# Six of eight blocks of the boundary unit computed ahead of the norm instead of eight

## The chip, the cores and the metric

The kernel runs on one core of a Trainium2 chip. The metric is the device time of one execution in microseconds (us), as the median of the runs. TensorE is called PE here, VectorE DVE, ScalarE ACT, GpSimd POOL and SyncE SP, as the profile calls them.

## The reference

The program is a small encoder trunk: two layers on 256 grid tokens and 16 meta tokens (272 columns), 1024 channels. Each layer is a half-step SwiGLU feed-forward block (FFN), a token mixer (neighbourhood attention in layer 0, differential attention in layer 1) and a second FFN, each between two norms:

```python
h = h + 0.5 * rmsnorm(swiglu(rmsnorm(h, g[0]), gate, up, down), g[1])
h = h + rmsnorm(mixer(rmsnorm(h, g[2])), g[3])
h = h + 0.5 * rmsnorm(swiglu(rmsnorm(h, g[4]), gate, up, down), g[5])
```

where `rmsnorm(x, g) = x * rsqrt(mean(x*x) + 1e-6) * g`, and `swiglu` is `(silu(x @ gate) * (x @ up)) @ down` with an inner width of 2816. Six sub-layers make five boundaries. At each, the output f of one sub-layer must be normed and added to h before the next sub-layer's first projection can use the new h.

## The kernel before

Channels lie on the 128 partitions, tokens on the free axis, so an activation is 8 blocks of 128 x 272. Every float32 matrix product is made of three passes on PE: each operand is split into a rounded high part and the rest (`whi`, `wlo` for weights, `xhi`, `xlo` for activations), and PE adds hi·hi, lo·hi and hi·lo. A *unit* is one 128-column slice of a weight matrix: 8 blocks, 24 matmuls (`mm3` for each block). There are 328 units; each is loaded by a DMA that SP issues, ACT makes its high part (line 126) and DVE its low part (line 132). Seven units can be held split (`W_BUFS`); `pump` splits the next one only if the unit seven before it was declared finished by `done()`.

The order on PE is the program's own everywhere; in the FFNs that holds for all engines, in the two attentions the other engines are ordered by a scheduler, which goes by the order of the code and by what each instruction waits for.

A boundary works so. The sub-layer's last product comes out in 8 blocks; `Post.feed` squares each one (ACT, line 268), scales it by its gain (`fg`, DVE), adds the squares up on POOL (`sqa`, line 273), and makes a split copy `fhi`, `flo` of it with the next gain. Meanwhile `input_hi` and `input_lo` make `xhi`, `xlo` from the old h. Since the norm is one factor per token, the first unit of the next sub-layer, here called unit 0, can be computed before it is known: once from the old h (pass A, into the bank `ab[0]`) and once from f (pass B, into `ab[1]`), 24 matmuls each. `enter` issues both. Between their blocks stand two steps of the norm: `post.rstd` (PE sums `sqa` over the channels into `st`, line 242; DVE makes v, line 250; POOL makes r, line 257) and `post.spread` (PE spreads r over the partitions, line 263). Then `post.add` goes over the 8 blocks: DVE scales f (line 350) and adds it to h (line 357), ACT makes the new `xhi` (line 277) and its square, DVE the new `xlo` (line 280), POOL adds the squares. PE's next five units follow as a *group*, block by block (`proj_group`, lines 200, 201 and 204: 15 matmuls for a block), so that block k only needs the new `xhi[k]` and `xlo[k]`. Ahead of the group's block 6 stands `ir.begin`, the sum of all eight new squares (line 242 again), and ahead of block 7 `ir.end` (line 263), which ACT copies out as `r2` (line 305). Unit 0's sum, pass A plus the scaled pass B, is formed by lines 383 to 385 (`u0`).

The five boundaries lie at 213 us (FFN to neighbourhood attention), 349 us (to an FFN), 558 us (FFN to FFN), 764 us (FFN to differential attention) and 902 us (to the last FFN, with 256 columns). The text calls them 1 to 5.

Of the kernel before, what the change touches and what calls it, by code (L numbers as in the profile page):

```python
# [38 lines left out]
W_BUFS = 7  # L39
RAW_BUFS = 5  # L40
WO_GROUP = 3
LEAD = 6
WARM = 8
FIRST = 2
# [3 lines left out]
def encoder_kernel(ctx, tc, xT, wall, gT, bqkvT, boT, sublnT, rpbP, metab, lam_p, rel,  # L48
# [16 lines left out]
    def nm(s):  # L65
        uid[0] += 1
        return f"{s}_{uid[0]}"
# [107 lines left out]
    def done(n=1):  # L175
        count["done"] += n
# [12 lines left out]
            mm3(acc[:, :n], w[0][:, k, :], w[1][:, k, :], ihi[:, k, :n], ilo[:, k, :n], k == 0, k == KB - 1)  # L189
        done()  # L190

    def proj_group(units, n_of, ihi, ilo, accs, hook):

        ws = [next_unit() for _ in units]
        for k in range(KB):
            if k in hook:
                hook[k]()
            for j in range(len(units)):
                n = n_of(units[j])
                nc.tensor.matmul(accs[j][:, :n], ws[j][0][:, k, :], ihi[:, k, :n], start=k == 0, stop=False)  # L200
                nc.tensor.matmul(accs[j][:, :n], ws[j][1][:, k, :], ihi[:, k, :n], start=False, stop=False)  # L201
            for j in range(len(units)):
                n = n_of(units[j])
                nc.tensor.matmul(accs[j][:, :n], ws[j][0][:, k, :], ilo[:, k, :n], start=False, stop=k == KB - 1)  # L204
        done(len(units))


    first = [load((2, 2, 4)) for _ in range(FIRST)]
# [98 lines left out]
    class Post:  # L307
# [8 lines left out]
        def open(self):  # L316
            self.cm = tc.tile_pool(name=nm("fx"), bufs=1, side="right")
            pool = self.cm.__enter__()
            self.fhi = pool.tile([P, KB, T], F32R, tag="fhi", name=nm("fhi"))
            self.flo = pool.tile([P, KB, T], F32R, tag="flo", name=nm("flo"))  # L320

        def feed(self, m, ps):
            n = self.n
            f = fg[:, m, :n]
            pump_hi() if m < KB - 1 else None
            if self.bias is None:
                sq = square(ps, n)
                nc.vector.tensor_scalar(out=f, in0=ps, scalar1=self.gain[:, m:m + 1], scalar2=None, op0=ALU.mult)
            else:
                sq = square(ps, n, bias=self.bias[:, m:m + 1])  # L330
                nc.vector.tensor_scalar(out=f, in0=ps, scalar1=self.bias[:, m:m + 1],
                                        scalar2=self.gain[:, m:m + 1], op0=ALU.add, op1=ALU.mult)
            self.acc = sq if m == 0 else add_squares(self.acc, sq, n)
            g = self.gain_next[:, m:m + 1]
            fhi = self.fhi[:, m, :n]
            nc.scalar.activation(fhi, f, AF.Copy, scale=g)
            pump_lo()
            nc.vector.scalar_tensor_tensor(out=self.flo[:, m, :n], in0=f, scalar=g, in1=fhi.bitcast(F32),
                                           op0=ALU.mult, op1=ALU.subtract)
# [23 lines left out]
    def enter(post, n_of, ab, rest):  # L363

        n0 = n_of(0)
        w = next_unit()
        for k in range(KB):
            if k == post.ready:  # L370
                post.rstd()
            mm3(ab[0][:, :n0], w[0][:, k, :], w[1][:, k, :], xhi[:, k, :n0], xlo[:, k, :n0], k == 0, k == KB - 1)
        for k in range(KB):
            if k == 2:
                post.spread()
            mm3(ab[1][:, :n0], w[0][:, k, :], w[1][:, k, :], post.fhi[:, k, :n0], post.flo[:, k, :n0],
                k == 0, k == KB - 1)
        done()
        post.cm.__exit__(None, None, None)
        ir = InputRstd(post.n_next)  # L380
        post.add(ir)
        u0 = nrm.tile([P, T], F32, tag="u0", name=nm("u0"), bufs=1)
        nc.scalar.copy(u0[:, :n0], ab[1][:, :n0])
        nc.vector.tensor_tensor(out=u0[:, :n0], in0=u0[:, :n0], in1=post.bc[:, :n0], op=ALU.mult)
        nc.vector.tensor_tensor(out=u0[:, :n0], in0=ab[0][:, :n0], in1=u0[:, :n0], op=ALU.add)
        pump(1)
        proj_group(range(1, 1 + len(rest)), n_of, xhi, xlo, rest, {6: ir.begin, 7: ir.end})
        pump(1)
        return [u0] + rest, ir

    def gains(l, i):
        return g_sb[:, l * 6 + i, :]
# [27 lines left out]
    def ffn(l, which, n, before, gain_next, n_next, extra=()):  # L420
        extra = list(extra)
        with all_banks(), tc.manual_schedule():
# [6 lines left out]
            with tc.tile_pool(name=nm("ffn"), bufs=1) as fp:  # L429
                mhi = fp.tile([P, FT, T], F32R, tag="mhi", name=nm("mhi"))  # L430
                mlo = fp.tile([P, FT, T], F32R, tag="mlo", name=nm("mlo"))

                def evac(f, pg, pu):
                    gt = ft.tile([P, T], F32, tag="gt", name=nm("gt"))
                    ut = ft.tile([P, T], F32, tag="ut", name=nm("ut"))
                    nc.vector.tensor_tensor(out=gt[:, :n], in0=pg[:, :n], in1=r2[:, :n], op=ALU.mult)  # L436
                    nc.vector.tensor_tensor(out=ut[:, :n], in0=pu[:, :n], in1=r2[:, :n], op=ALU.mult)
                    nc.scalar.activation(gt[:, :n], gt[:, :n], AF.Silu)  # L438
                    pump_hi()
                    nc.vector.tensor_tensor(out=ut[:, :n], in0=gt[:, :n], in1=ut[:, :n], op=ALU.mult)  # L440
                    pump_lo()
                    nc.scalar.copy(mhi[:, f, :n], ut[:, :n])
                    nc.vector.tensor_tensor(out=mlo[:, f, :n], in0=ut[:, :n],
                                            in1=mhi[:, f, :n].bitcast(F32), op=ALU.subtract)
                    pump(1)

                with tc.tile_pool(name=nm("fft"), bufs=2) as ft:
                    pools["tmp"] = ft
                    for f in range(3):
                        evac(f, accs[2 * f], accs[2 * f + 1])  # L450
                    for f in range(3, FT):
                        a, b = acc_tile(), acc_tile()
                        proj(a, n, xhi, xlo)
                        proj(b, n, xhi, xlo)
                        evac(f, a, b)
                        if extra:
                            extra.pop(0)()
                    if which == 0:
                        nc.scalar.activation(warm, ones, AF.Exp)
                        if l == 1:  # L460
                            lambda_scalar()
                if gain_next is None:
                    with tc.tile_pool(name="last", bufs=1) as lp:
                        last_down(lp, mhi, mlo)
                    return None
                post = Post(n, half_gains(l, 1 if which == 0 else 5), None, gain_next, n_next, 6)
                post.open()
                w = None
                for m in range(KB):
                    ps = acc_tile()  # L470
                    for f in range(FT):
                        idx = m * FT + f
                        if idx % KB == 0:
                            if w is not None:
                                done()
                            w = next_unit()
                            if extra:
                                extra.pop(0)()
                            if idx % FT < 16:
                                pump(1)  # L480
                        mm3(ps[:, :n], w[0][:, idx % KB, :], w[1][:, idx % KB, :],
                            mhi[:, f, :n], mlo[:, f, :n], f == 0, f == FT - 1)
                    post.feed(m, ps[:, :n])
                    if m < KB - 1:
                        for i in range(m + m // 6, m + 1 + (m + 1) // 6):
                            input_hi(i, gain_next, n_next)
                            input_lo(i, gain_next, n_next)
                assert not extra
                done()
            return post  # L490
# [204 lines left out]
    def natten(l, b4, before, gain_next, n_next):  # L695
        with ExitStack() as outer, ExitStack() as inner:
# [172 lines left out]
                    single.append((i, lambda p=pairs, go=go: go(p)))  # L869
            for u in range(6):  # L870
                stage(u, accs[u])
            post = Post(T, gains(l, 3), bo_sb, gain_next, n_next, 7)
            fl = Filler(range(6, 24), lambda u: T, stage, ohi, olo, post)
            pipeline(fl, steps, (1, 3, 6), single)
            nc.gpsimd.tensor_tensor(out=warm[:NMETA], in0=meta["L"][:, 0, 0:1], in1=cur["sm"][:NMETA, 0:1], op=ALU.add)
# [5 lines left out]
    class Filler:  # L881
# [5 lines left out]
        def run(self, units, n_of, staging, ohi, olo, post):  # L887
# [13 lines left out]
            for k in range(KB):  # L901
                for j in range(WO_GROUP):
                    mm3(self.outs[j][:, :n], ws[j][0][:, k, :], ws[j][1][:, k, :],
                        ohi[:, k, :n], olo[:, k, :n], k == 0, k == KB - 1)
                    if k < KB - 1 or j < WO_GROUP - 1:
                        yield
                if k < KB - 1:
                    for i in range(k + k // 6, k + 1 + (k + 1) // 6):
                        input_hi(i, post.gain_next, post.n_next)
                        input_lo(i, post.gain_next, post.n_next)  # L910
            done(WO_GROUP)
            yield

# [41 lines left out]
    def diff_attention(l, b4, before, gain_next, n_next):  # L955
# [3 lines left out]
        with ExitStack() as outer, ExitStack() as inner:  # L959
# [122 lines left out]
            nc.vector.tensor_scalar(out=r2s[0], in0=ir.r2[:, :NG], scalar1=0.125, scalar2=None, op0=ALU.mult)  # L1082
            for u in range(6):
                stage(u, accs[u])
            post = Post(NG, gains(l, 3), None, gain_next, n_next, 7)
# [113 lines left out]
```

## Time and profile before

| | |
|---|---|
| median of 3 runs | 1104.18 us (1103.87 to 1104.58) |
| profiled execution | 1104.21 us |
| its span, first to last instruction | 1102.4 us |
| PE busy | 1089.8 us (99%), 8492 matmuls |
| DVE busy | 779.9 us (71%) |
| ACT busy | 612.6 us (56%) |
| POOL busy | 131.9 us (12%) |
| mean granted TensorE clock | 0.995 |

The profiled execution takes 1.8 us more than its span, which lie around it. Busy times are shares of the span. Matmuls overlap: one is shown with some 0.29 us, but the next begins 0.125 us after it, so the starts are to be read, not the lengths.

### The profile page before, as it was taken

Reading aid. Unit: us, or ns where it says so; the run is one execution under the profiler, and the core shown is the slowest. Engines: PE = TensorE matmul, PEld = TensorE weight load, DVE = VectorE, ACT = ScalarE, POOL = GpSimd, SP = SyncE. Lnnn points to the kernel's source line nnn. Section 1 sums busy time; section 2 is a strip of 40 time slices with the busy share of each in tenths; the row PEclk is TensorE's granted clock in tenths of the full one; section 3 lists DMA queues with packets and bytes.
Section 4 is the critical chain, followed back from the end, with each engine's and each line's share of the span. In section 5 each row is a group of like instructions: output and inputs, shape, how many; then the busy total and the mean of one; then the engine's idle time right before and its main releaser. Section 6 shows DMA issues by size and latency. Waiting matters only on the chain.

```text
span 1102.4 us, 22240 instructions
## 1 busy us (share of the span) xinstructions
PE 1089.8 (99%) x8492; PEld 1057.4 (96%) x8492; DVE 779.9 (71%) x1669; ACT 612.6 (56%) x1398; POOL 131.9 (12%) x234
## 2 busy tenths in 40 slices
PE   8999999999999999999999999999999999999997
PEld 8999999999989999999999999999999999999986
DVE  6676868687677887675578766666887778877642
ACT  4554655476666564455546544554677865654541
POOL 4000001152222200000020000001321122000000
PEclk8999999999999999999999999999999999999999
DMA  7589985525334375695526555555253343755551
GB/s 252 178 151 212 275 228 168 176 73 182 110 97 135 110 224 172 178 239 192 175 69 210 192 185 164 181 184 172 77 173 96 111 140 113 241 184 185 184 167 39
DMA packets 64956, 181.79 MB, mean 165 GB/s; under 512 B 13960, under 2 KB 22192, under 8 KB 64848
## 3 DMA queue, kind: packets, MB, share of 16 engines
q1 hardware_dynamic: 64848, 180.35, 54.4%
q8 instruction: 67, 1.10, 0.4%
q14 instruction: 41, 0.34, 0.1%
HBM read 179.21 MB, written 1.20 MB: 164 GB/s over the span
## 4 chain that ended last, share of the span: by engine, by line
PE 90%; DVE 6%; issue 2%; ACT 1%; POOL 0%; DMA 0%; SPq 0%; POOLq 0%; DVEq 0%; ACTq 0%
PE acc L179 16%; PE acc L181 15%; PE acc L180 15%; PE att L179 10%; PE att L181 9%; PE att L180 9%; DVE xlo L280 1%; DVE wlo L132 1%; DVE h L357 1%; PE acc L200 1%; PE acc L204 1%; PE acc L509 1%; PE acc L511 1%; PE acc L510 1%; PE acc L201 1%
## 5 line engine op out<-in xcount | busy, mean ns | idle before, releaser
L132 DVE TENSOR_TENSOR wlo<-raw,whi 128x512 fp32r<-128x512 f32 (+1 forms) x660 | 439.0, 704 | 64.3 <-ACT whi L126 60.9
L126 ACT CAST whi<-raw 128x512 fp32r<-128x512 f32 (+1 forms) x660 | 374.4, 613 | 107.4 <-issue 44.3
L179 PE MATMUL acc<-xhi,whi 128*128 128x272 f32 (+1 forms) x1016 | 299.2, 294 | 0.0
L181 PE MATMUL acc<-xlo,whi 128*128 128x272 f32 (+1 forms) x1016 | 291.9, 287 | 0.0
L180 PE MATMUL acc<-xhi,wlo 128*128 128x272 f32 (+1 forms) x1016 | 291.0, 286 | 0.0
L179 PEld LDWEIGHTS acc<-xhi,whi 128*128 128x128 f32 x1016 | 191.4, 188 | 5.6 <-issue 3.7
L180 PEld LDWEIGHTS acc<-xhi,wlo 128*128 128x128 f32 x1016 | 191.5, 188 | 0.2 <-DVE wlo L132 0.2
L181 PEld LDWEIGHTS acc<-xlo,whi 128*128 128x128 f32 x1016 | 191.3, 188 | 0.0
L179 PE MATMUL att<-xhi,whi 128*128 128x272 f32 (+1 forms) x560 | 161.1, 288 | 0.0
L181 PE MATMUL att<-xlo,whi 128*128 128x272 f32 (+1 forms) x560 | 160.9, 287 | 0.0
L180 PE MATMUL att<-xhi,wlo 128*128 128x272 f32 (+1 forms) x560 | 160.3, 286 | 0.0
L438 ACT ACTIVATE gt<-gt 128x272 f32<-128x272 f32 (+1 forms) x88 | 37.7, 428 | 143.7 <-DVE gt L436 143.7
L179 PEld LDWEIGHTS att<-xhi,whi 128*128 128x128 f32 x560 | 105.5, 188 | 0.7 <-issue 0.7
L181 PEld LDWEIGHTS att<-xlo,whi 128*128 128x128 f32 x560 | 105.5, 188 | 0.0
L180 PEld LDWEIGHTS att<-xhi,wlo 128*128 128x128 f32 x560 | 105.4, 188 | 0.0
L179 PE MATMUL acc<-mhi,whi 128*128 128x272 f32 x286 | 82.8, 290 | 0.0
L181 PE MATMUL acc<-mlo,whi 128*128 128x272 f32 x286 | 82.3, 288 | 0.0
L180 PE MATMUL acc<-mhi,wlo 128*128 128x272 f32 x286 | 82.3, 288 | 0.0
L273 POOL TENSOR_TENSOR sqa<-sqa,sq 128x272 f32<-128x272 f32 (+1 forms) x66 | 55.6, 842 | 166.7 <-ACT sq L268 163.8
L179 PE MATMUL att<-mhi,whi 128*128 128x272 f32 x242 | 70.1, 290 | 0.0
L181 PE MATMUL att<-mlo,whi 128*128 128x272 f32 x242 | 69.7, 288 | 0.0
L180 PE MATMUL att<-mhi,wlo 128*128 128x272 f32 x242 | 69.6, 288 | 0.0
(248 smaller groups left out, 1970.2 us busy)
## 6 DMA issues: line engine op xcount, KB each, us to landing
raw<-wall SPq DMA_DIRECT2D x326, 512.0 KB, 4.0
bias<-tab SPq DMA_DIRECT2D x8, 320.0 KB, 9.9
bias<-tab SPq DMA_DIRECT2D x8, 256.0 KB
h<-xT SPq DMA_DIRECT2D x3, 272.0 KB, 4.6
out<-ht SPq DMA_DIRECT2D x3, 256.0 KB
raw<-wall SPq DMA_DIRECT2D x4, 128.0 KB, 3.1
raw<-wall SPq DMA_DIRECT2D x2, 256.0 KB
grow<-glast SPq DMA_DIRECT2D x1, 512.0 KB, 5.1
```

What stands on the lines that cost most here:

```text
L126: nc.scalar.copy(split[i][0][:, sl], raw[i][:, sl])
L132: nc.vector.tensor_tensor(out=wlo[:, sl], in0=raw[i][:, sl], in1=whi[:, sl].bitcast(F32), op=ALU.subtract)
L179: nc.tensor.matmul(ps, whi_k, mhi, start=first, stop=False)
L180: nc.tensor.matmul(ps, wlo_k, mhi, start=False, stop=False)
L181: nc.tensor.matmul(ps, whi_k, mlo, start=False, stop=last)
L200: nc.tensor.matmul(accs[j][:, :n], ws[j][0][:, k, :], ihi[:, k, :n], start=k == 0, stop=False)
L201: nc.tensor.matmul(accs[j][:, :n], ws[j][1][:, k, :], ihi[:, k, :n], start=False, stop=False)
L204: nc.tensor.matmul(accs[j][:, :n], ws[j][0][:, k, :], ilo[:, k, :n], start=False, stop=k == KB - 1)
L273: nc.gpsimd.tensor_tensor(out=t[:, :n], in0=acc[:, :n], in1=sq[:, :n], op=ALU.add)
L280: nc.vector.scalar_tensor_tensor(out=xlo[:, m, :n], in0=h[:, m, :n], scalar=gain[:, m:m + 1], in1=xhi[:, m, :n].bitcast(F32), op0=ALU.mult ...
L357: nc.vector.tensor_tensor(out=h[:, m, :n], in0=h[:, m, :n], in1=fg[:, m, :n], op=ALU.add)
L438: nc.scalar.activation(gt[:, :n], gt[:, :n], AF.Silu)
```

## The change

`AHEAD = 6`. Passes A and B cover blocks 0 to 5 alone, 18 matmuls each. Blocks 6 and 7 of unit 0 are computed once, from the new h, in the group: its blocks 6 and 7 have 18 matmuls instead of 15, and they go on adding into the bank of pass A. `fhi`, `flo` and the old `xhi`, `xlo` are no longer made for blocks 6 and 7. `rstd` stands two blocks earlier in pass A (before block 4 after an FFN, 5 after an attention, instead of 6 and 7), `spread` before block 3 of pass B instead of 2. `done()` for unit 0 comes with the group's, and the last addition of `u0` stands behind the group.

```diff
-    def proj_group(units, n_of, ihi, ilo, accs, hook):
-        ws = [next_unit() for _ in units]
+    def proj_group(units, n_of, ihi, ilo, accs, hook, begun=()):
+        parts = [(w, acc, n, AHEAD) for w, acc, n in begun]
+        parts += [(next_unit(), acc, n_of(u), 0) for u, acc in zip(units, accs)]
         for k in range(KB):
             if k in hook:
                 hook[k]()
...
+            here = [p for p in parts if k >= p[3]]
+            for w, acc, n, _ in here:
+                nc.tensor.matmul(acc[:, :n], w[0][:, k, :], ihi[:, k, :n], start=k == 0, stop=False)
+                nc.tensor.matmul(acc[:, :n], w[1][:, k, :], ihi[:, k, :n], start=False, stop=False)
+            for w, acc, n, _ in here:
+                nc.tensor.matmul(acc[:, :n], w[0][:, k, :], ilo[:, k, :n], start=False, stop=k == KB - 1)
+        done(len(parts))
...
             self.acc = sq if m == 0 else add_squares(self.acc, sq, n)
+            if m >= AHEAD:
+                pump_lo()
+                return
...
-        for k in range(KB):
+        for k in range(AHEAD):
             if k == post.ready:
                 post.rstd()
-            mm3(ab[0][:, :n0], ..., k == 0, k == KB - 1)
-        for k in range(KB):
-            if k == 2:
+            mm3(ab[0][:, :n0], ..., k == 0, False)
+        for k in range(AHEAD):
+            if k == 3:
                 post.spread()
-            mm3(ab[1][:, :n0], ..., k == 0, k == KB - 1)
-        done()
+            mm3(ab[1][:, :n0], ..., k == 0, k == AHEAD - 1)
...
         nc.vector.tensor_tensor(out=u0[:, :n0], in0=u0[:, :n0], in1=post.bc[:, :n0], op=ALU.mult)
+        pump(1)
+        proj_group(range(1, 1 + len(rest)), n_of, xhi, xlo, rest, {6: ir.begin, 7: ir.end}, [(w, ab[0], n0)])
         nc.vector.tensor_tensor(out=u0[:, :n0], in0=ab[0][:, :n0], in1=u0[:, :n0], op=ALU.add)
-        pump(1)
-        proj_group(range(1, 1 + len(rest)), n_of, xhi, xlo, rest, {6: ir.begin, 7: ir.end})
         pump(1)
```

What the change does to the order is shown at three places (the changed kernel's lines stand one to six further on). First PE at boundary 3, where the group comes to block 6; `st` is the sum of the squares, the bank `acc_7313`, then `acc_7277`, that of unit 1. Before:

```order
L204 MATMUL att_7317<-xlo,whi_7268 128x272
L242 MATMUL st_7542<-ones,sqa_7436 128x1 x3
L200 MATMUL acc_7313<-xhi,whi_7130 128x272
L201 MATMUL acc_7313<-xhi,wlo_7131 128x272
L200 MATMUL att_7314<-xhi,whi_7162 128x272
```

and now:

```order
L206 MATMUL att_7281<-xlo,whi_7234 128x272
L244 MATMUL st_7493<-ones,sqa_7388 128x1 x3
L203 MATMUL acc_7275<-xhi,whi_7070 128x272
L204 MATMUL acc_7275<-xhi,wlo_7071 128x272
L203 MATMUL acc_7277<-xhi,whi_7100 128x272
```

Unit 0 (`acc_7275`, the bank of pass A) now leads the block behind the sum; the same stands at the other four boundaries.

Next DVE at the same boundary, behind `post.add`; `u_586` is `u0`, v the second sum's, `gt` the FFN's first evacuation. Before:

```order
L384 TENSOR_TENSOR u_586_7440<-u_586_7440,st_7336 128x272
L385 TENSOR_TENSOR u_586_7440<-acc_7311,u_586_7440 128x272
L132 TENSOR_TENSOR wlo_7445<-raw_7136,whi_7444 128x512 x2
L250 TENSOR_SCALAR v_7543<-st_7542 128x3
L132 TENSOR_TENSOR wlo_7586<-raw_7168,whi_7585 128x512 x2
L436 TENSOR_TENSOR gt_7601<-u_586_7440,r_590_7568 128x272
```

and now:

```order
L388 TENSOR_TENSOR u_586_7392<-u_586_7392,st_7294 128x272
L133 TENSOR_TENSOR wlo_7396<-raw_7106,whi_7395 128x512 x2
L252 TENSOR_SCALAR v_7494<-st_7493 128x3
L391 TENSOR_TENSOR u_586_7392<-acc_7275,u_586_7392 128x272
L133 TENSOR_TENSOR wlo_7544<-raw_7138,whi_7543 128x512 x2
L440 TENSOR_TENSOR gt_7559<-u_586_7392,r_590_7522 128x272
```

The addition that frees the bank of pass A has moved from ahead of the second sum to behind it, and reads what the group's last block writes.

Last ACT at boundary 4, from the copy of `r2` on; `hi` are the high parts of the first query (x256) and the first key (x272). Before:

```order
L305 COPY r_732_10120<-st_10094 128x272
L987 CAST hi_10157<-qk_10155 128x256
L126 CAST whi_10214<-raw_9766 128x512 x2
L126 CAST whi_10301<-raw_9796 128x512 x2
L987 CAST hi_10163<-qk_10161 128x272
```

and now:

```order
L307 COPY r_732_10060<-st_10031 128x272
L127 CAST whi_10081<-raw_9678 128x512 x2
L127 CAST whi_10158<-raw_9721 128x512 x2
L127 CAST whi_10245<-raw_9748 128x512
L989 CAST hi_10101<-qk_10099 128x256
L127 CAST whi_10245<-raw_9748 128x512
L127 CAST whi_10267<-raw_9780 128x512 x2
L127 CAST whi_10307<-raw_9939 128x512
L989 CAST hi_10107<-qk_10105 128x272
```

Ahead of the first key's high part stand nine casts of weights instead of four. Two of the nine are those of the unit that takes over unit 0's buffers (`whi_10081`); before, they stood within `post.add`. At boundary 1 two casts have moved in the same way.

## Rows read from the trace of the kernel before

**Rows 1.** The page: TensorE's busy time, its granted clock in 40 slices, the chain.

```profile
PE 1089.8 (99%) x8492; PEld 1057.4 (96%) x8492; DVE 779.9 (71%) x1669; ACT 612.6 (56%) x1398; POOL 131.9 (12%) x234
...
PEclk8999999999999999999999999999999999999999
...
PE 90%; DVE 6%; issue 2%; ACT 1%; POOL 0%; DMA 0%; SPq 0%; POOLq 0%; DVEq 0%; ACTq 0%
```

**Rows 2.** The waits of PE: total us, times, longest us.

```profile
PE st L242 <- POOL sqa L273: 1.7, 4, 0.6
...
PE att L1076 <- DVE A L1017: 1.0, 1, 1.0
```

**Rows 3.** Timeline of PE at boundary 3: start us, length us, instruction, [idle before].

```profile
558.53 0.28 PE L179 MATMUL acc<-xhi,whi 128*128 128x272 f32 x1
...
560.79 0.28 PE L242 MATMUL st<-ones,sqa 128*128 128x1 f32 x2
...
562.97 0.27 PE L263 MATMUL st<-ident,r 128*128 128x128 f32 x1
...
565.55 0.29 PE L200 MATMUL acc<-xhi,whi 128*128 128x272 f32 x1
...
577.30 0.27 PE L242 MATMUL st<-ones,sqa 128*128 128x1 f32 x1 [0.28 <-POOL sqa L273]
...
582.17 0.28 PE L179 MATMUL acc<-xhi,whi 128*128 128x272 f32 x1
```

**Rows 4.** Timeline of POOL, DVE and ACT at boundary 3.

```profile
559.33 0.78 POOL L273 TENSOR_TENSOR sqa<-sqa,sq 128x272 f32<-128x272 f32 x1 [7.26 <-ACT sq L268]
...
561.79 0.86 POOL L257 TENSOR_TENSOR r<-v,mhalf 128x3 f32<-128x3 f32 x1 [1.68 <-DVE v L250]
...
563.49 0.44 DVE L350 TENSOR_TENSOR fg<-fg,st 128x272 f32<-128x272 f32 x1 [1.78 <-PE st L263]
...
564.50 0.53 ACT L277 ACTIVATE xhi<-h,g_sb 128x272 fp32r<-128x272 f32 x1 [4.23 <-DVE h L357]
...
576.48 0.77 POOL L273 TENSOR_TENSOR sqa<-sqa,sq 128x272 f32<-128x272 f32 x1 [1.38 <-ACT sq L268]
```

**Rows 5.** Timeline of ACT, POOL and PE at boundary 2.

```profile
350.43 0.53 ACT L336 ACTIVATE fhi<-fg,g_sb 128x272 fp32r<-128x272 f32 x1 [0.93 <-DVE fg L331]
...
351.48 0.77 POOL L273 TENSOR_TENSOR sqa<-sqa,sq 128x272 f32<-128x272 f32 x1 [0.91 <-ACT sq L268]
...
352.31 0.27 PE L242 MATMUL st<-ones,sqa 128*128 128x1 f32 x1 [0.52 <-POOL sqa L273]
...
354.33 0.32 PE L263 MATMUL st<-ident,r 128*128 128x128 f32 x1
```

**Rows 6.** Timeline of PE at boundary 5.

```profile
904.70 0.28 PE L242 MATMUL st<-ones,sqa 128*128 128x1 f32 x2
...
906.24 0.32 PE L263 MATMUL st<-ident,r 128*128 128x128 f32 x1
```

**Rows 7.** Timeline of POOL, PE and ACT at boundary 1.

```profile
213.72 0.78 POOL L273 TENSOR_TENSOR sqa<-sqa,sq 128x272 f32<-128x272 f32 x1
...
215.13 0.28 PE L242 MATMUL st<-ones,sqa 128*128 128x1 f32 x2
...
217.31 0.27 PE L263 MATMUL st<-ident,r 128*128 128x128 f32 x1
...
219.06 0.53 ACT L277 ACTIVATE xhi<-h,g_sb 128x272 fp32r<-128x272 f32 x1 [4.09 <-DVE h L357]
...
219.89 0.29 PE L200 MATMUL acc<-xhi,whi 128*128 128x272 f32 x1
...
220.55 0.36 ACT L383 COPY u<-att 128x272 f32<-128x272 f32 x1
```

**Rows 8.** Timeline of ACT, DVE and PE behind boundary 4.

```profile
786.28 0.41 ACT L987 CAST hi<-qk 128x256 fp32r<-128x256 f32 x1 [1.02 <-DVE qk L981]
786.59 2.18 ACT L126 CAST whi<-raw 128x512 fp32r<-128x512 f32 x4
788.67 0.41 ACT L987 CAST hi<-qk 128x272 fp32r<-128x272 f32 x1
...
789.12 0.44 DVE L989 TENSOR_TENSOR lo<-qk,hi 128x272 fp32r<-128x272 f32 x1
...
790.21 0.40 PE L179 MATMUL att<-hi,hi 64*128 64x272 f32 x2
```

More of the change, by code (lines that the diff above doesn't have):

```diff
@@ L41 @@
 WO_GROUP = 3
+AHEAD = 6
 LEAD = 6
@@ L197, in proj_group @@
                 hook[k]()
[L198 to L205, printed above, removed]
+            here = [p for p in parts if k >= p[3]]
[5 more added lines that the diff above has]
+        done(len(parts))
     first = [load((2, 2, 4)) for _ in range(FIRST)]
@@ L318, in open @@
             pool = self.cm.__enter__()
-            self.fhi = pool.tile([P, KB, T], F32R, tag="fhi", name=nm("fhi"))
-            self.flo = pool.tile([P, KB, T], F32R, tag="flo", name=nm("flo"))
+            self.fhi = pool.tile([P, AHEAD, T], F32R, tag="fhi", name=nm("fhi"))
+            self.flo = pool.tile([P, AHEAD, T], F32R, tag="flo", name=nm("flo"))
         def feed(self, m, ps):
@@ L368, in enter @@
         w = next_unit()
-        for k in range(KB):
+        for k in range(AHEAD):
             if k == post.ready:
                 post.rstd()
-            mm3(ab[0][:, :n0], w[0][:, k, :], w[1][:, k, :], xhi[:, k, :n0], xlo[:, k, :n0], k == 0, k == KB - 1)
-        for k in range(KB):
-            if k == 2:
+            mm3(ab[0][:, :n0], w[0][:, k, :], w[1][:, k, :], xhi[:, k, :n0], xlo[:, k, :n0], k == 0, False)
+        for k in range(AHEAD):
+            if k == 3:
                 post.spread()
             mm3(ab[1][:, :n0], w[0][:, k, :], w[1][:, k, :], post.fhi[:, k, :n0], post.flo[:, k, :n0],
-                k == 0, k == KB - 1)
-        done()
+                k == 0, k == AHEAD - 1)
         post.cm.__exit__(None, None, None)
@@ L465, in ffn @@
                     return None
-                post = Post(n, half_gains(l, 1 if which == 0 else 5), None, gain_next, n_next, 6)
+                post = Post(n, half_gains(l, 1 if which == 0 else 5), None, gain_next, n_next, 4)
                 post.open()
@@ L483, in ffn @@
                     post.feed(m, ps[:, :n])
[L484 to L487, printed above, removed]
+                    if m < AHEAD:
+                        input_hi(m, gain_next, n_next)
+                        input_lo(m, gain_next, n_next)
                 assert not extra
@@ L871, in natten @@
                 stage(u, accs[u])
-            post = Post(T, gains(l, 3), bo_sb, gain_next, n_next, 7)
+            post = Post(T, gains(l, 3), bo_sb, gain_next, n_next, 5)
             fl = Filler(range(6, 24), lambda u: T, stage, ohi, olo, post)
@@ L906, in run @@
                         yield
[L907 to L910, printed above, removed]
+                if k < AHEAD:
+                    input_hi(k, post.gain_next, post.n_next)
+                    input_lo(k, post.gain_next, post.n_next)
             done(WO_GROUP)
@@ L1084, in diff_attention @@
                 stage(u, accs[u])
-            post = Post(NG, gains(l, 3), None, gain_next, n_next, 7)
+            post = Post(NG, gains(l, 3), None, gain_next, n_next, 5)
             fl = Filler(range(6, 24), nof, stage, ohi, olo, post)
```

## The prediction

> **What bounds the kernel now.** I read the page first [rows 1]: PE is busy 99% of the span and its clock is full from the second slice on, so at first sight every matmul taken away is time won. The chain of waits bears that out for 90% of the span, but gives 6% to DVE. The list of PE's waits says where [rows 2]: four of its waits, 1.7 us in all, are for the sum of squares `sqa`, and one of 1.0 us for DVE behind boundary 4. So I went to the timeline of each boundary and read starts. At boundary 3 [rows 3] pass A starts at 558.53 and the first sum at 560.79, 18 matmuls later: 0.126 us each. The spread of r starts at 562.97, the group at 565.55, the second sum at 577.30 after a wait, the next unit at 582.17. Beside it [rows 4] runs the norm: POOL's last square is added by 560.11, r is ready at 562.65, 1.86 us after the first sum began, the first scaling starts at 563.49, the new `xhi[0]` is done at 565.03, and the last new square at 577.25. The reader is to see how closely the two fit: `xhi[0]` is ready 0.5 us before the group needs it, and the second sum waits for POOL, though 90 matmuls stand before it. Pass B is not work that PE could simply drop; it is what PE does while DVE and ACT make the first block of the new h.
>
> **The change, step by step.** Matmuls first: each boundary loses 6 in pass A and 6 in pass B and gains 6 in the group, so 6 go, 30 in all: 30 x 0.126 = 3.8 us, if no wait grew. By the Trainium skill, TensorE: Matmul & The Clock Gate, section Back-to-back issue gap, matmuls follow each other after N/2.4 + 2.5 ns, an estimate of 0.116 us at 272 columns and 3.5 us for the 30; the trace shows 0.126, and goes before it.
>
> *Boundary 3.* The first sum now stands behind 12 matmuls, at 558.53 + 12 x 0.126 = 560.04, but must wait for POOL, 560.11 plus the 0.05 that a release takes (577.25 to 577.30): 560.16, 0.63 earlier. From there to the spread were 12 matmuls in 2.18 us, now 15: 2.18 + 0.38 = 2.56, which still covers the 1.86 of v and r. The spread starts at 562.72, only 0.25 earlier. Behind it 18 matmuls, 2.58 us, led to the group; now 9, 2.58 - 1.13 = 1.45 us. But `xhi[0]` was done 2.06 us after the spread began, and nothing in that chain (spread, scaling, addition, cast) is shortened. So the group starts at 562.72 + 2.11 = 564.83: PE waits 0.66 us there. The 8 blocks of `post.add` set the second sum: it began 577.30 - 562.97 = 14.33 us after the spread, so now at 577.05; PE, with 90 matmuls from 564.83, is there at 576.17 and waits 0.88 us. From the second sum to the next unit were 4.87 us; the 6 matmuls of unit 0 now stand here, where they have no cover: 0.75 us. And the next unit needs the bank of pass A, which DVE's addition frees: the last matmul on it starts 6 x 0.126 = 0.75 us before the group's end, and its length (0.29), a start of DVE (0.07), an addition like that of `fg` (0.44) and the release (0.05) are 0.85, a wait of 0.1. What is queued behind the addition on DVE are two splits of weights and the first evacuation; the unit split there is needed 24 matmuls later, 3 us, against some 2 us for its casts and splits. Boundary 3: -0.25 + 0.75 + 0.1 = +0.60 us.
>
> *Boundary 2.* Here the first sum was late: it waited for POOL, POOL had been idle 0.91 us for the last square, and on ACT that stood behind `fhi` of block 6, which itself waited for DVE [rows 5]. That `fhi` goes, so POOL can be up to 0.91 earlier; I take 0.8, as its addition before must end first. The sum starts at 351.51. To the spread were 2.02 us with 9 matmuls, now 12, as at boundary 3 before: 2.18 to 2.3. The spread starts 0.57 earlier, and `post.add` with it. The second sum is one of the four waits, so the rest is as above: -0.57 + 0.75 + 0.1 = +0.28 us.
>
> *Boundary 5* [rows 6]: the first sum had no wait and moves with its 6 matmuls, 0.7 us earlier; to the spread 12 matmuls instead of 9: +0.36. With its 256 columns (0.118 us a matmul): -0.35 + 0.70 + 0.1 = +0.45 us.
>
> *Boundary 1* [rows 7]: the first sum moves from 215.13 to POOL's end, 214.55; with 15 matmuls to the spread that starts at 217.11 (-0.20). `xhi[0]` was done 2.28 us after the spread. ACT now does the copy of pass B ahead of it (before, it stood at 220.55, behind two blocks): pass B ends some 1.4 us behind the spread, the copy starts at 218.8 and holds ACT 0.26, so `xhi[0]` is done at 219.6 and the group starts at 219.66, 0.23 earlier. The second sum does not wait here. So -0.23 + 0.75 = +0.52 us; the next unit takes the bank of pass B, which is free. Then the weight casts: seven units are held, and unit 0 is now finished with the group, so the two casts of the unit that takes its buffers, 0.55 us each [rows 8], fall behind the group, ahead of the first query and key. I put 0 to 1.0 us on PE, and take 0.3.
>
> *Boundary 4* is boundary 1 again up to the group's end, +0.52. But behind it ACT is full. Before, the first key's high part stood behind one cast and four weight casts, at 788.67, its low part was done at 789.56, and PE used it at 790.21, 0.65 us later [rows 8]. Now nine weight casts stand ahead, the first of which can only start when unit 0's last matmul is through, about 786.4: 786.4 + 9 x 0.545 + 0.3 = 791.6 for the key's high part, 792.5 for its low part. PE comes at 790.73 and waits 1.8 us. In return the later wait of 1.0 us for DVE [rows 2] goes, since PE comes that much later and DVE's work does not move as far. I count +1.0 (from -0.5, if the casts find gaps, to 2.0, if that wait stays in part), so +1.5 us.
>
> The sum is 0.8 + 0.3 + 0.6 + 1.5 + 0.45 = +3.65 us. The 20 instructions saved on DVE and 20 on ACT count for nothing but boundary 2's 0.8 us: elsewhere PE does not wait for these engines. No DMA is added, and SP's and POOL's orders stay. The profiled execution took 1104.21 us, its span 1102.4 and 1.8 around it; the median, 1104.18, is the same. So 1107.8 us.
>
> **Rivals.** *The matmuls are what counts* (faster): if the new `xhi[0]` came within 1.45 us of the spread, and `post.add` kept up with PE, all 3.8 us would be won: 1100.4. For it: PE's 99%. Against it: 2.06 and 2.28 us in rows 3, 4 and 7, and the second sum's four waits. It decides from the point where the group's first matmul waits less than 0.1 us. 5%. *The earlier start pays the late matmuls back* (no change): the first sum moves by more than I think at boundaries 1, 3 and 4, and the casts at 4 only fill the wait of 1.0 us: 0.4 for each of 1 and 4, 0.2 for each other, +1.4 us: 1105.6. For it: the first sum itself is 0.6 us earlier everywhere. Against it: it then stands behind 3 more matmuls. 24%. *The casts block both attentions* (slower): 2.5 us at boundary 4, 1.5 at boundary 1, the FFNs as forecast, +6 us: 1110. For it: ACT takes its queue in order, and the first of the casts waits for PE. 12%. *The clock falls*: PE's waits become longer, and the slice in which the page shows 8 tenths instead of 9 or more lost about 0.2 x 27.6 = 5.5 us; once more that would be 1113. Against it: the four waits before left the clock full in all later slices. 2%. The rule is in the Trainium skill, TensorE: Matmul & The Clock Gate, section HAM oscillation: waits between bunches of matmuls can put the array back to half its clock; by this trace waits of 0.6 us don't.
>
> **How the numbers follow.** The forecast has 57%, around 1107.8, by its bounds 1106.0 to 1109.3. With the rivals on both sides down to one in five left out: 1105.0 to 1110.2. A measurement of this kernel can tell some 0.2%, 2.2 us, from no change, so slower means over 1106.4. That holds for nearly all of the forecast and the two slow rivals, 69%; no change for the third rival and a tail of the forecast, 26%; faster 5%.
>
> **What would show it.** In the profile after: a wait of 0.5 to 0.8 us of the group's first matmul for ACT's `xhi` at boundaries 2, 3 and 5; the waits for `sqa` ahead of the second sum near 0.9 us instead of 0.3 to 0.6; the spread at boundary 3 0.25 us earlier; PE waiting for DVE's `lo` behind boundary 4, and no wait any more for A. If the groups start without a wait, or the stretch from pass A to the next unit at boundary 3 is under 23.6 us, the forecast is wrong; if only the attention stretches differ, its size is.

## The result, and the profile after

The changed kernel takes 1111.59 us (median, 1111.06 to 1112.31) against 1104.18: a ratio of 1.0068 (1.0053 to 1.0082), 7.4 us slower. The forecast was 3.65 us slower; the time lies above its range, which ended at 1110.2. The profiled execution has a span of 1109.8 us, 7.4 more than before, so the trace has the whole loss in it; its last matmul is 7.0 us later.

The page still shows a PE that is all but full, and 30 matmuls fewer:

```profile
PE 1087.9 (98%) x8462; PEld 1053.2 (95%) x8462; DVE 772.4 (70%) x1649; ACT 604.6 (54%) x1378; POOL 132.4 (12%) x234
...
PE 90%; DVE 6%; issue 1%; ACT 1%; POOL 1%; DMA 0%; SPq 0%; POOLq 0%; DVEq 0%; ACTq 0%
```

PE's waits (total us, times, longest us) answer to [rows 2]:

```profile
PE acc L203 <- ACT xhi L279: 3.5, 6, 0.9
...
PE st L244 <- POOL sqa L275: 2.3, 5, 0.6
...
PE att L180 <- ACT hi L989: 1.3, 1, 1.3
PE att L1078 <- DVE A L1019: 0.9, 1, 0.9
...
PE att L755 <- DVE nmx L759: 0.7, 1, 0.7
...
PE att L182 <- DVE lo L991: 0.3, 1, 0.3
```

New are the five waits for the new `xhi[0]` (the sixth is at the program's start), one ahead of each group. The wait for A, which was to go, is still there (1.0 before), and three waits inside the attentions have come.

To see where the time went I took the start of the same matmul in both traces, ahead of and behind each boundary:

| boundary | forecast, us | up to and with the group | behind it, in the attention |
|---|---|---|---|
| 1 | +0.8 | +0.89 | +0.96 |
| 2 | +0.28 | +0.26 | |
| 3 | +0.60 | +0.72 | |
| 4 | +1.5 | +0.46 | +3.40 |
| 5 | +0.45 | +0.19 | |

The forecast stands for both columns together. With 0.16 ahead of boundary 1 the parts make these 7.0 us. The three FFN boundaries are what was forecast (1.17 for 1.33), and so nearly are the group parts of 1 and 4 (1.35 for 1.04). 4.4 us lie where 1.3 were put: in the first 20 us of the two attentions.

PE at boundary 3 (start, length, instruction, [idle before]; [rows 3] are its counterparts):

```profile
560.79 0.28 PE L180 MATMUL acc<-xhi,whi 128*128 128x272 f32 x1
...
562.42 0.27 PE L244 MATMUL st<-ones,sqa 128*128 128x1 f32 x1
...
565.07 0.27 PE L265 MATMUL st<-ident,r 128*128 128x128 f32 x1
...
567.18 0.40 PE L203 MATMUL acc<-xhi,whi 128*128 128x272 f32 x1 [0.50 <-ACT xhi L279]
...
579.28 0.27 PE L244 MATMUL st<-ones,sqa 128*128 128x1 f32 x1 [0.52 <-POOL sqa L275]
...
585.07 0.36 PE L180 MATMUL acc<-xhi,whi 128*128 128x272 f32 x1
```

The group still starts 2.11 us behind the spread, as `xhi[0]` allows; PE has only 9 matmuls for that time and waits. The second sum is 14.21 us behind the spread (14.33 before). From pass A to the next unit are 24.28 us, 0.64 more, and 0.72 three matmuls later, where the table takes it.

Behind boundary 4, DVE and ACT (the second spread is at 787.42; before it was at 784.35):

```profile
788.37 0.30 DVE L1084 TENSOR_SCALAR r2s<-r 128x256 f32<-128x256 f32 x1 [2.86 <-ACT r L307]
789.53 0.42 DVE L391 TENSOR_TENSOR u<-att,u 128x256 f32<-128x256 f32 x1 [0.87 <-PE att L206]
789.88 0.43 DVE L977 TENSOR_TENSOR vs<-acc,r 128x272 f32<-128x272 f32 x1
790.22 1.28 DVE L133 TENSOR_TENSOR wlo<-raw,whi 128x512 fp32r<-128x512 f32 x2
791.43 0.64 DVE L983 TENSOR_TENSOR qk<-u,r2s 128x256 f32<-128x256 f32 x1
...
789.53 2.71 ACT L127 CAST whi<-raw 128x512 fp32r<-128x512 f32 x5 [1.20 <-PE att L206]
792.14 0.40 ACT L989 CAST hi<-qk 128x256 fp32r<-128x256 f32 x1
792.45 2.18 ACT L127 CAST whi<-raw 128x512 fp32r<-128x512 f32 x4
794.53 0.42 ACT L989 CAST hi<-qk 128x272 fp32r<-128x272 f32 x1
```

and PE there:

```profile
795.00 0.39 PE L180 MATMUL att<-hi,hi 64*128 64x272 f32 x1 [1.31 <-ACT hi L989]
...
795.83 0.39 PE L182 MATMUL att<-lo,hi 64*128 64x272 f32 x1 [0.31 <-DVE lo L991]
...
805.85 0.30 PE L1078 MATMUL att<-ident,A 128*128 128x128 f32 x1 [0.89 <-DVE A L1019]
```

Before, the product that makes the first query from u0 (`qk`) stood ahead of the group's end; the next unit's first matmul is the last row:

```profile
785.29 0.29 DVE L1082 TENSOR_SCALAR r2s<-r 128x256 f32<-128x256 f32 x1 [2.50 <-ACT r L305]
785.62 0.62 DVE L981 TENSOR_TENSOR qk<-u,r2s 128x256 f32<-128x256 f32 x1
...
786.52 0.28 PE L179 MATMUL att<-xhi,whi 128*128 128x256 f32 x1
```

That is 1.27 us behind the second spread and 0.9 before the next unit; now it is 4.00 behind the spread. DVE is idle from `r2s` to 789.53 and ACT to the same moment: u0 and the weight buffers that the next casts need both wait for unit 0's last matmul, near the group's end. Then the two splits of a weight unit stand ahead of the query. Everything on the line that follows (query, key, exponentials, A) is late by as much.

### The profile page after: what moved, and what is told of

Its sections match the earlier page's. It is cut to its first block, busy times and chain, and to the rows that moved or that the text cites. A ratio compares the mean times of both kernels' runs of the same rounds, so it can differ in the third digit from the quotient of the medians.

```text
span 1109.8 us, 22146 instructions
## 1 busy us (share of the span) xinstructions
PE 1087.9 (98%) x8462; PEld 1053.2 (95%) x8462; DVE 772.4 (70%) x1649; ACT 604.6 (54%) x1378; POOL 132.4 (12%) x234
## 4 chain that ended last, share of the span: by engine, by line
PE 90%; DVE 6%; issue 1%; ACT 1%; POOL 1%; DMA 0%; SPq 0%; POOLq 0%; DVEq 0%; ACTq 0%
PE acc L180 16%; PE acc L182 15%; PE acc L181 15%; PE att L180 10%; PE att L182 9%; PE att L181 9%; DVE wlo L133 1%; DVE h L362 1%; DVE xlo L282 1%; PE acc L203 1%; PE acc L206 1%; PE acc L204 1%; PE acc L512 1%; PE acc L514 1%; PE acc L513 1%
```

## The experiments

Each was timed beside the kernel before (1104.05 to 1104.25 us there). Two changed kernels that differ by 1 to 2 us lie within the intervals of their ratios, some 1.3 us either way, so there I go by the traces. I read one number from every trace: the time from the second spread to the 150th matmul behind it, less the same in the kernel before (20.34 us at boundary 4, 19.12 at 1). It leaves out the late matmuls, counts waits and a lowered clock, and is called the loss below; the changed kernel has 3.35 at boundary 4 and 1.09 at boundary 1. Beside it stands when the first query's product starts on DVE behind the second spread (1.27 before, 4.00 after).

**Where: one kind of boundary alone.** The number of blocks ahead was made a property of each boundary.

```
ffn_only:  blocks ahead: 6 entering an FFN, 8 entering an attention
att_only:  blocks ahead: 8 entering an FFN, 6 entering an attention
```

> The change at boundaries 2, 3 and 5 alone (the ones that enter an FFN); boundaries 1 and 4 stay at eight blocks. Theory (most of the loss lies in the attention stages, because unit 0 holds its weight buffers until the group ends and the casts move behind it): the stretches of the trace of the changed kernel give 0.26 + 0.72 + 0.19 = 1.2 us here, so 1105.4 us. Rival (every boundary pays about the same, 7.4 / 5 = 1.5 us, for its late matmuls and the wait ahead of the group): 4.4 us more, 1108.6.

> The change at boundaries 1 and 4 alone (the ones that enter an attention). Theory: the trace's stretches give 1.84 + 3.86 = 5.7 us, so 1109.9 us, with PE waits of 1.0 us at boundary 1 for DVE's nmx, and of 1.6 and 0.6 us at boundary 4 for the first key's hi and lo. Rival (every boundary pays about the same): 3.0 us more, 1107.2.

Measured: 1105.29 us, ratio 1.0010 (1.0001 to 1.0019), and 1109.17, ratio 1.0048 (1.0036 to 1.0061). The two sum to 6.0 of 7.4 us, and the attentions make 4.9 of it; the rest is left open, the intervals being 2 to 3 us wide. So the loss is not spread evenly over the five.

**Why: the held buffers.** My forecast had put the attention's price on the weight buffers that unit 0 keeps until the group ends. One run takes that away from the changed kernel, one adds it to the kernel before.

```
release:  + nc.scalar.copy(keep[i], w[i][:, AHEAD:, :])   # at the spread
          + done()                                        # behind pass B
hold:     + two matmuls of 16 columns on w[0], w[1] behind the group
```

> The changed kernel, but the two late blocks of unit 0's weights are copied by ACT into buffers of their own, so that unit 0's weight buffers come free behind pass B as before. The late matmuls, the late addition of u0 and everything else stay. Theory (held buffers): the 3.4 us behind boundary 4 and the 1.0 us behind boundary 1 go, 1111.6 - 4.4 = 1107.2 us. Rival (the first query is what is late: u0 is added only behind the group, so the first hi on ACT falls behind the casts whoever holds the buffers): nothing changes by more than the copies cost, 1111.6 us.

> The kernel before, all eight blocks ahead, but two short matmuls of 16 columns that read unit 0's weights stand behind the group at each boundary, so that its buffers are held until the group ends as in the changed kernel; their result is not used. u0 is added early as before. The ten short matmuls cost 0.05 to 0.1 us each, 0.5 to 1.0 us. Theory (held buffers): with the 4.4 us of boundaries 1 and 4, 1104.2 + 4.4 + 0.7 = 1109.3 us. Rival (the late u0): 1104.2 + 0.7 = 1104.9 us.

Measured: release 1110.33 us, 1.3 less than the changed kernel (its runs, 1110.02 to 1110.40, lie below all of that kernel's); hold 1106.78, ratio 1.0035 (1.0023 to 1.0047), with runs from 1106.19 to 1111.13, the trace being of the lowest. Both times lie between theory and rival. In the traces release has a loss of 2.37 at boundary 4 and 1.21 at 1, hold 0.95 and 0.40. Both say the same: the held buffers are worth 1.0 us at boundary 4, and little at 1. As the main cause they fall. In hold it is one wait, 1.1 us longer than before:

```profile
800.87 0.30 PE L1078 MATMUL att<-ident,A 128*128 128x128 f32 x1 [2.17 <-DVE A L1019]
```

**Why: the late u0.** The kernel before, with u0's last addition held back to the group's end:

```
late_u0:  - nc.vector.tensor_tensor(out=u0, in0=ab[0], in1=u0, op=add)  # ahead of the group
          + matmul(ab[1][:, :16], ident, xhi[:, 7, :16])                # behind it
          + u0[:, :1] = ab[1][:, :1] * 0 + u0[:, :1]; then the addition
```

> The kernel before, all eight blocks ahead and the weight buffers free early, but at boundaries 1 and 4 the addition that finishes u0 waits for a short matmul that stands behind the group (16 columns, times zero), so that u0, the first query, is as late as in the changed kernel. Theory (the late first query is the larger part of the loss: with the buffers released the stretches behind the group were still 2.4 us longer at boundary 4 and 1.2 at boundary 1): 1104.25 + 3.6 + 0.1 = 1107.9 us. Rival (what is left after the buffers is the price of the late matmuls on PE and of the wait ahead of the group, not of u0): 1104.4 us.

Measured: 1110.62 us, ratio 1.0061 (1.0049 to 1.0074). The query's product starts at 4.33, the losses are 3.62 and 2.81. The new dependence also keeps the next unit's bank busy, which the changed kernel does not do:

```profile
790.05 0.38 PE L179 MATMUL att<-xhi,whi 128*128 128x256 f32 x1 [0.41 <-DVE u L391]
...
795.05 0.39 PE L179 MATMUL att<-hi,hi 64*128 64x272 f32 x1 [1.15 <-ACT hi L992]
...
805.76 0.30 PE L1081 MATMUL att<-ident,A 128*128 128x128 f32 x1 [2.15 <-DVE A L1022]
```

So it overstates, at boundary 1 by more than twice, but a late u0 alone, with buffers free and no late block, makes a loss of this size.

**Another unit last.** If u0 is late because it is the first query, let the second value be the one that is late.

```
v_first, v_first_rel:  - w = next_unit()                  # unit 0, the first query
                       + w = ws[5]                        # the sixth, the second value
```

> The changed kernel, but at boundaries 1 and 4 the unit that is computed ahead, and finished last, is the sixth of the six (the second value) and not the first (the first query). Its buffers are still held until the group ends. Theory (late first query): the 3.6 us go, 1111.6 - 3.6 = 1108.0 us, with no wait of PE for the first key's hi above 0.5 us. Rival (late matmuls and held buffers alone): 1111.6 us, since neither changes.

> The run with the copied weights of unit 0 (1110.3 us), with the sixth unit ahead in place of the first query at boundaries 1 and 4, so that neither the buffers nor the first query are late. Theory: 1110.3 - 3.6 = 1106.7 us, which is the kernel before, 1104.25, plus what PE's own part of the five boundaries costs (0.5 + 0.3 + 0.7 + 0.5 + 0.2 = 2.2 us). Rival (the first query's lateness is harmless): 1110.3 us.

Measured: 1110.15 and 1110.52 us, both far from the expectation. The reason is in the order: the first query is now a unit of the group, so its product starts at 2.47 and 2.49 us, at the group's end, and the losses at boundary 4 are 2.11 and 2.40. In v_first PE has one wait there, of 1.0 us, and a lowered clock (last section); v_first_rel has its loss without that. The kernel before has more than a query that isn't last: its product starts 0.9 us before the group's end.

**Order and load of the engines.** Four runs: the first query and key moved forward on DVE; one unit's splits on POOL; and DVE or ACT work added to the kernel before.

```
prio:        + with tc.high_priority(): u0's addition, stage(0), stage(1)
pool_after:  + wlo of the unit behind the group on gpsimd (boundary 4)
dve_load:    + 2 x nc.vector.tensor_tensor, 128x512, behind the second spread
act_load:    + 3 x nc.scalar.copy, 128x272, behind the second spread
```

> The changed kernel, with u0's addition and the first query and key of both attentions moved forward in the order of DVE (and with them ACT): at boundary 4 the query's product then stands ahead of the two weight splits of 1.28 us instead of behind them. Nothing is left out. Theory (load of DVE and ACT): the same work is only ordered otherwise, the first key's wait shrinks and the later wait for A grows; 0 to 1 us less, 1111.0 us. Rival (the lateness of the first query and key alone): 1.3 us of boundary 4 and some of boundary 1 go, 1109.8 us.

> The changed kernel, with the two lo splits of the one weight unit that takes unit 0's buffers, behind boundary 4, on POOL instead of DVE (1.28 us of DVE's time there; POOL is idle for 15 of the 18 us from the second spread to the transposes of A). Theory (load of DVE): 0.6 to 1.3 us less, 1110.6 us. Rival (ACT's casts, which stay, set the first key): no change, 1111.6 us.

> The kernel before with two more DVE operations of 128x512 (about 0.65 us each) at the start of both attentions; their result is not used. Theory (the start of an attention is bound by DVE and ACT together, which are busy some 90% of the time from the second spread to the first transposes, so that whatever is moved there from beside the group costs nearly its own length): 1.0 to 1.3 us more at boundary 4 and 0.5 to 1.3 at boundary 1, 1106.2 us. Rival (only the first query and key matter; before, the key was ready 0.65 us ahead of its use): at most 0.3 us more, 1104.4 us.

> The kernel before with three more copies of 128x272 on ACT (about 0.4 us each, 1.2 in all) at the start of both attentions; their result is not used. DVE's 1.37 us more cost 0.5 us at boundary 1 and 2.6 at boundary 4. Theory (at boundary 1 it is ACT that has no slack: it was idle for only 1.0 of the 11.0 us from the second spread to the transposes): 1.0 us or more at boundary 1, and 1.0 to 2.5 at boundary 4, 1106.5 us. Rival (DVE alone bounds both starts): at most 0.4 us in all, 1104.4 us.

Measured: prio 1109.76 us, 1.8 less than the changed kernel and the time of its rival: product at 2.80, losses 1.71 and 1.00. What its theory named is in the trace too: PE's two waits for the first key shrink from 1.6 to 0.4 us, and the wait for A grows from 0.9 to 1.75. pool_after 1110.55 with a loss of 3.22 at boundary 4: its key is even later, and the boundary gains next to nothing. The 1.0 us by which its median is lower is not from there: its runs (1110.46 to 1112.00) overlap with the changed kernel's, and of the 0.5 us by which its trace is shorter, 0.4 is a shorter wait for the second sum at boundary 5. dve_load 1107.38, ratio 1.0029 (1.0017 to 1.0040): 0.54 at boundary 1 and 2.58 at boundary 4, where 1.0 is the longer wait for A

```profile
798.76 0.33 PE L1081 MATMUL att<-ident,A 128*128 128x128 f32 x1 [2.03 <-DVE A L1022]
```

and the rest a lowered clock behind it (below). act_load 1105.36, ratio 1.0012 (1.0003 to 1.0020): 1.62 more at boundary 4, but 0.42 less at boundary 1, where with the extra copies the weight casts and splits stand further back. At boundary 4 added work shows in PE's waits, 1.0 us for 1.37 on DVE and, as loss, 1.62 for 1.2 on ACT; at boundary 1 ACT's added 1.2 us came with another order and a shorter stretch, so no engine is simply full there. My guess of ACT there is refuted.

**Do buffers and order add up?** The copied weights and the forward order in one kernel, prio_rel:

> The run with copied weights of unit 0 (1110.3 us: buffers free early) and, with it, u0's addition and the first query and key moved forward in DVE's order as in the run that measured 1109.8 us. Theory (two separate terms at boundary 4, 1.7 us for the order and 1.0 for the held buffers, and a rest of 0.7 for the late start): both go, 1109.8 - 1.2 = 1108.6 us, with 0.7 us left behind the group at boundary 4 and 1.0 to 1.2 at boundary 1. Rival (the two are one wait, seen twice): 1109.8 us.

Measured: 1110.43 us; product at 2.82, losses 2.21 and 1.18. They do not add up: freeing the buffers on top of the order does not lower prio's loss of 1.71. With either or both, the product starts at the group's end, since u0 is not there sooner, and 1.7 to 2.4 us stay.

**Taking the lateness back.** In the last block of the group, unit 0's three matmuls go first, so that u0 is complete 1.8 us before the group ends; alone, and with copied weights and forward order.

```
u0_first:     if k == KB - 1: mm3(unit 0, block 7); then the other units as before
u0_first_pr:  the same on prio_rel
```

> The changed kernel, with unit 0's three matmuls of block 7 at the head of that block of the group and not among the other units', so that u0 is complete about 15 matmuls, 1.9 us, before the group ends and its addition, the scaling and the cast of the first query can run beside the group again; its buffers come free as much earlier. The same matmuls are computed. Theory (what is lost behind boundaries 1 and 4 is that nothing of the attention's first work can start before the group ends): 1.5 us or more of boundary 4 and 0.5 to 1.0 of boundary 1 come back, 1109.3 us. Rival (the rest is the late matmuls' own price and the order that the new lateness of everything brings): 1111.3 us.

> The same order of block 7 together with the copied weights (buffers free behind pass B) and the first query and key forward in DVE's order: all three ways in which the change makes the attention's start late, taken back as far as the late matmuls allow. Theory: only PE's own part of the five boundaries is left, 2.2 us, and 0.3 to 0.7 behind boundary 4: 1106.8 us. Rival (the copies and the order alone left 1110.4 us, and the start stays late): 1110 us.

Measured: 1107.88 us, ratio 1.0033 (1.0021 to 1.0046), 3.7 less than the changed kernel; and 1105.06 us, ratio 1.0008 (0.9999 to 1.0017), which is not clear of no change. In u0_first's trace the last matmul comes 3.2 us sooner than in the changed kernel's: 2.75 of it is won behind boundaries 1 and 4, and 0.6 at the three FFN boundaries, where the next unit no longer waits for the bank of pass A. Query and buffers both come sooner in it, so it does not tell the two apart. The pair that does is prio_rel and u0_first_pr: the buffers are free early in both, the order in the code is forward in both, and they differ only in those three matmuls. The loss falls from 2.21 to 0.02 at boundary 4 and from 1.18 to -0.19 at boundary 1, the time by 5.4 us. u0_first_pr is 1.7 us under its expectation: in its trace PE's own part of the five boundaries is 1.2 us and not 2.2, boundary 5 being 0.5 shorter than in the kernel before by a shorter wait for the second sum. In u0_first_pr DVE and ACT stand behind boundary 4 (second spread at 786.01) as they did before:

```profile
786.91 0.42 DVE L403 TENSOR_TENSOR u<-att,u 128x256 f32<-128x256 f32 x1 [2.80 <-PE att L182]
787.25 0.28 DVE L1099 TENSOR_SCALAR r2s<-r 128x256 f32<-128x256 f32 x1
787.57 0.64 DVE L998 TENSOR_TENSOR qk<-u,r2s 128x256 f32<-128x256 f32 x1
...
788.30 0.41 ACT L1004 CAST hi<-qk 128x256 fp32r<-128x256 f32 x1 [1.37 <-PE acc L213]
788.61 2.18 ACT L127 CAST whi<-raw 128x512 fp32r<-128x512 f32 x4
790.70 0.41 ACT L1004 CAST hi<-qk 128x272 fp32r<-128x272 f32 x1
```

Four casts, not nine, stand ahead of the key again [rows 8]. The traces for boundary 4, without those of the two added loads and of the kernels that leave it as it was:

| kernel | first query's product, us behind the spread | first key's lo done | loss |
|---|---|---|---|
| before | 1.27 | 5.21 | 0 |
| u0_first_pr | 1.56 | 5.57 | 0.02 |
| hold | 1.27 | 5.83 | 0.95 |
| u0_first | 2.75 | 6.84 | 1.42 |
| prio | 2.80 | 7.14 | 1.71 |
| v_first | 2.47 | 6.57 | 2.11 |
| prio_rel | 2.82 | 7.19 | 2.21 |
| release | 2.82 | 7.19 | 2.37 |
| v_first_rel | 2.49 | 7.19 | 2.40 |
| pool_after | 2.80 | 8.95 | 3.22 |
| att_only | 4.00 | 8.35 | 3.35 |
| changed | 4.00 | 8.35 | 3.35 |
| late_u0 | 4.33 | 8.32 | 3.62 |

The loss goes with the first key rather than with the query itself: pool_after has the query sooner than the changed kernel, the key later, and nearly the same loss.

**Better than both?** From the waits that the kernel before has itself: the first sum one block earlier, and A's chain forward.

```
early_sum:  - ready 6 (FFN to next), spread at k == 2    + ready 5, spread at k == 1
            - ready 7 (boundary 5)               + ready 6, spread at k == 1
best:       the same, + with tc.high_priority(): weights of the first head
```

> The kernel before with the first sum and the spread of r one block earlier at boundaries 1, 3, 4 and 5, all eight blocks ahead. Theory (the chain from the spread to the second sum sets the end of an FFN boundary, not the matmuls): boundary 3 gains the 0.38 us that the spread is earlier, boundary 5 about 0.2 (its first sum is then held by POOL), 1 and 4 nothing: 1104.25 - 0.6 = 1103.7 us, the waits for the second sum at 3 and 5 shorter by as much. Rival (PE's matmuls set it): 1104.25 us.

> The kernel before, eight blocks ahead, with the first sum and the spread one block earlier at boundaries 1, 3, 4 and 5 (alone: boundaries 3 and 4 were 0.4 us shorter, but the whole within noise), and with the first head's weights (sums, reciprocals, A) moved forward in DVE's and ACT's order behind boundary 4, where PE waits 1.3 us for A. Theory: 0.4 to 0.8 us less than before from the sums and 0.5 to 1.0 from A, 1102.9 us. Rival (A's wait comes back as another wait of the same stage): 1103.8 us.

Measured: 1104.03 us, ratio 1.0000 (0.9991 to 1.0008), and 1103.39, ratio 0.9994 (0.9985 to 1.0003). The trace of best shows the wait for A down from 1.0 [rows 2] to 0.43,

```profile
796.77 0.33 PE L1078 MATMUL att<-ident,A 128*128 128x128 f32 x1 [0.43 <-DVE A L1019]
```

and the last matmul 0.75 us earlier, but the medians do not tell either from the kernel before.

## Why the prediction was wrong, step by step

*PE's own part was right.* At boundaries 2, 3 and 5 the group's first matmul waits 0.66 us (its start is 0.78 behind the last of pass B, less the pitch), where 0.66 was worked out; the second sum waits 0.7 to 0.8 for 0.88, and the next unit 0.2 for the bank of pass A, for 0.1. At boundary 2 the first sum starts 0.84 us earlier against pass A, for 0.8: the `fhi` behind which the last square stood was the reason, as read in [rows 5]. ffn_only confirms the sum, 1.0 us for 1.3. At boundary 1 the group starts 0.04 us later instead of 0.23 earlier, since POOL's last square came 0.2 later than by [rows 7]; that is most of the 0.4 us of error there.

*The step that failed* is the one on boundary 4: "In return the later wait of 1.0 us for DVE [rows 2] goes, since PE comes that much later and DVE's work does not move as far." The +1.0 us counted there measured +3.40. What stands ahead of that sentence came out: the key's low part was put at 792.5 and PE's wait at 1.8; it was done at 795.77, which is 792.8 less the 2.98 by which the boundary had started later, and PE waited 1.95 (two waits, less the pitch). But DVE's work did move as far. In the changed kernel A's wait stayed and PE ran at half clock ahead of it; in att_only, without the slow clock, there are two waits for A, 2.3 us over the pitch for 1.2 before; the loss is 3.35 both times. The same held at boundary 1, where I put 0.3 us on the casts: 0.96 are lost there, in a wait for DVE.

*Why DVE moved* I had not seen at all. I priced u0's late addition by the bank that it frees for an FFN's next unit (0.1 us) and not by who reads u0: in an attention it is the first query, and the kernel before began it 0.9 us before the group's end, right behind 2.5 us in which DVE was idle. I named the casts on ACT and the held buffers instead. release and hold give the buffers 1.0 us of 3.35; late_u0 shows that the late query alone makes such a loss, and u0_first_pr that with query, buffers and order back in their places nothing is left (0.02 at boundary 4, 0.2 gained at 1). Shown, then: the lateness of u0 is the main cause (2.37 us are left in release, where the buffers are free, and 2.2 us go from prio_rel to u0_first_pr, where only u0 comes sooner), the held buffers the lesser, and they overlap. How much each has in the changed kernel is not shown exactly, because DVE's and ACT's order differs from one of these kernels to the next: prio won 1.64 us of the loss by the order alone, with u0 as late as before.

*The rivals.* "The casts block both attentions" had the nearest time (1110) and got 12%; it put 2.5 us at boundary 4 and 1.5 at boundary 1, where 3.40 and 0.96 were lost behind the group, and its mechanism was the lesser one. That the matmuls are what counts fell as argued: 30 fewer, and each boundary slower. That the earlier start pays the late matmuls back failed with the wait for A, which stayed. The clock did fall (last section), at a chance of 2%; its price of 5.5 us was read from a whole tenth on the page, while the trace grants 0.88 on average over that slice of 27.56 us, which is 3.4 us.

## What to carry to other kernels

When an operation is moved behind a group, price it by every reader of its result, in the stage that follows too, and look at what else the readers' engines can do at that moment: here an addition of 0.4 us, by which a query came 2.7 us later, was the larger part of 3.4 us. The query behind it had run while DVE and ACT had little else to do; now it stood in a stretch in which they are busy 88% and 85% of the time (kernel before, second spread to the wait for A). A wait far down a chain isn't won back by arriving later when the late work is on the same chain. Giving such a result back its place needs no undoing of the change: putting three matmuls first in a block was worth 3.7 us, most of it behind the two boundaries at which the result was late for an attention.

## What was not expected of the hardware

The granted clock fell behind boundary 4 of the changed kernel (columns: stretch, its length, PE busy, granted clock, share of the DMA engines, GB/s):

```profile
796.00:797.00 1.00, 1.00 (x8) 1.00 0.82 266
797.00:798.00 1.00, 1.00 (x8) 0.63 0.86 242
798.00:799.00 1.00, 1.00 (x7) 0.50 0.55 213
799.00:800.00 1.00, 1.00 (x6) 0.50 0.32 98
800.00:801.00 1.00, 1.00 (x8) 0.67 0.94 348
801.00:802.00 1.00, 1.00 (x11) 1.00 0.23 90
```

0.50 is the 1.2 GHz level; matmuls then followed each other after 0.22 us. 1.7 us of full clock were missing in all. PE had waited 1.31 and 0.31 us just before. The same fall behind boundary 4, 1.7 us, is in the traces of v_first, pool_after and dve_load, and in none of the others, though att_only has the same two waits, and hold, late_u0, prio and u0_first waits of 1.75 to 2.2 us at A. By the Trainium skill, TensorE: Matmul & The Clock Gate, section HAM oscillation, waits between bunches of matmuls can put the array back to half its clock. The four traces with the fall agree: it came behind waits of 1.0 to 2.0 us. The others show that such a wait alone doesn't decide it. In the changed kernel it cost little, since PE ran into the wait for A anyway: att_only has the same loss without it. In dve_load it came behind that wait, and is most of what 1.37 us of added DVE work cost there.
